# Two-layer hybrid decoder step: PSUM banks of the second mixer dealt 3/3 instead of 4/2, and out-projection norms worked on in PSUM

## The chip, the cores and the metric

The kernel runs on one core of a Trainium2 chip. Its time is device microseconds of one launch, as the median of several runs. The engines are called TensorE (PE), VectorE (DVE), ScalarE (ACT), GpSimd (POOL) and SyncE (SP, which issues the loads and stores).

## What is computed

One step of a decoder of two layers over a prompt of 1024 rows and 8 sample rows, width 1024, all in float32. Layer 0 mixes tokens with forgetting attention (12 heads of 64), layer 1 with differential attention (6 pairs of heads) and rotary positions; in both, four heads attend to a memory. An output projection and a feed-forward part follow, each with a norm before and one behind. The reference, cut to what the change touches:

```python
for i in range(DEPTH):
    xn_p = rms_norm(h_p, g_pre_mix[i])
    ...                                    # layer 1: differential attention
    q, k, v, qm_p = diff_project(xn_p, w_in_diff[j], pos_p)   # q and k with rope
    o_p = diff_head_norm(diff_prompt(q, k, v, lam), g_subln[j], lam_init)
    ...                                    # the same for the sample rows, over a paged cache
def finish_layer(h, o_self, qm, mk, mv, g_post_mix, w_out, g_pre_ffn, g_post_ffn, w_gate_up, w_down):
    merged = jnp.concatenate([o_self, memory_attend(qm, mk, mv)], axis=-1)
    h = h + rms_norm(merged @ w_out, g_post_mix)
    u = rms_norm(h, g_pre_ffn) @ w_gate_up
    f = (silu(u[..., :D_FF]) * u[..., D_FF:]) @ w_down
    return h + rms_norm(f, g_post_ffn)
```

## The kernel before

Every float32 product is made of three: weights and activations are split into a rounded part and a rest (`h_w`, `l_w`; `hi` on ScalarE, L170, and `lo` on VectorE or POOL, L173), and `mm3` runs rounded x rounded, rounded x rest and rest x rounded over eight slices of 128, that is 24 matmuls for each projection tile of 128 columns by a third of the rows (384, 384 and 264).

PSUM has eight banks of 512 columns. In the mixers they are dealt by `MIXER` (L40): one tile of two banks (`s2`, for scores wider than 512), four single banks (`t`: scores up to 512, all transposes, attention outputs `av`, rows turned for the cache), and two for projections (`g`). Tiles of one tag take its banks in turn, so a tile waits until the tile that had the bank before it has been read. In the FFNs another deal holds (`s2` 1, `t` 2, `g` 4); the out projection (`wo`) runs there as well.

The mixer of layer 1 goes head pair by head pair, six in all. For a pair it projects q, k and v, three thirds each (`g`, L1167); between the matmuls, at each call of `beat`, TensorE runs one piece of the attention of the pair before: scores (`s_d`), transposes of the weights (`tp_d`), and the product with v (`av_d`). TensorE's order is written out by `Pinned`: each matmul is pinned behind the one before it in the program. The other engines' orders come from the framework's scheduler.

After a q or k projection VectorE and POOL rotate the tile in place (L998 to L1002), ScalarE copies the rounded part (`qq` L403, `kk` L170) and VectorE writes the rest (`ql` L406, `kk` L173); these are the last readers of the bank. A v tile is read by one ScalarE copy alone (L1175). For attention VectorE takes the row maxima (`nm_d`, L447), ScalarE the exponentials (`p_d`, L463), VectorE merges the two maps (`p_d`, L552), ScalarE drains transposes (`pt_d`, L475), products (`ao_d`, L1191) and turned rows (`tn`, L1137 and L1139). POOL works through the pages of the sample rows' cache beside it all (`kp`, L616).

`finish_tile` (L371) closes a tile of 128 rows: TensorE turns it into the two-bank tile `yp` (eight transposes), ScalarE sums its squares (L338), copies it to SBUF as `yn` (L382, which calls L170), VectorE and POOL form the inverse root (L329, L333), VectorE scales it (L387), adds it to the residual `h` (L388), and, where another part follows, norms it for that (L345) before TensorE turns it back as `xt`. Names begin with `o` for the out projection (18 of them, nine in each layer) and with `f` for the FFN; then come the layer, the third and the tile in it (`y_o002`).

Of the kernel before, what the change touches and what calls it, by code (L numbers as in the profile page):

```python
# [9 lines left out]
F32 = mybir.dt.float32  # L10
# [3 lines left out]
ALU = mybir.AluOpType  # L14
# [3 lines left out]
D = 1024  # L18
# [18 lines left out]
OUTS = 5  # L37
WAIT = 2.5
RD = 9.0
MIXER = {"s2": 1, "t": 4, "g": 2}  # L40
EAGER, IDLE = -200, 400
FFN = {"s2": 1, "t": 2, "g": 4}
THIRDS = ((0, 3, 384), (3, 3, 384), (6, 2, 264))
# [52 lines left out]
class Step:  # L96
# [274 lines left out]
    def finish_tile(self, pool, acc, o, ti, hsrc, hdst, g_post, g_pre, x, name, wait, row=None):  # L371

        nc = self.nc
        r = self.rows(ti)
        h = self.load_h(pool, ti, hsrc, f"h_{name}")
        y = pool.tile([128, D], F32, name=f"yn_{name}", tag="nat")
        if row is None:
            yp = self.b2(f"y_{name}")
            for k in range(8):
                self.pe.transpose(yp[:r, k * 128 : (k + 1) * 128], acc(k)[:, o : o + r], self.ident)  # L380
            ss = self.sumsq(pool, yp[:r], r, y, f"sy_{name}")
            self.hi(y[:r], yp[:r])  # L382
            row = y
        else:
            ss = self.sumsq(pool, row[:r], r, y, f"sy_{name}")
        rs = self.rstd(pool, ss[:r], r, D, f"ry_{name}")
        nc.vector.scalar_tensor_tensor(y[:r], row[:r], rs[:r], g_post[:r], op0=ALU.mult, op1=ALU.mult)  # L387
        nc.vector.tensor_tensor(h[:r], h[:r], y[:r], op=ALU.add)  # L388
        nc.sync.dma_start(hdst(ti), h[:r])
        if x is not None:  # L390
            self.norm(pool, h, r, g_pre, y, name)
            yield wait
            self.to_x(y, r, lambda tv, k0: [(tv, x[:, k0 : k0 + 4])], o, name)
# [647 lines left out]
    def mixer(self, l, xs, st, begin):  # L1041


        nc, io, tc = self.nc, self.io, self.tc
        w_in = io["w_in_fox"][0] if l == 0 else io["w_in_diff"][0]
        self.lag, self.ahead, self.vshare = LAG[l], AHEAD[l], VSHARE[l]
        with ExitStack() as cx:
            self.phase(cx, f"pm{l}", MIXER)
            wp = Weights(self.wpool)
            bufs = {"u4": 12, "p": 2, "pS": 2, "G": 1, "tt": 1}  # L1050
            if l == 1:
# [8 lines left out]
            rs = [{} for _ in range(6)]  # L1060
# [649 lines left out]
```

## Time and profile before

| | |
|---|---|
| runs | 3060.4, 3060.92, 3066.18 us; median 3060.92 us |
| the profiled execution | 3070.34 us, its span 3068.5 us |
| TensorE | busy 2806.3 us (91%), 17567 matmuls |
| VectorE | busy 2068.0 us (67%) |
| ScalarE | busy 1767.4 us (58%) |
| POOL | busy 1107.1 us (36%) |
| mean granted clock of TensorE | 0.963 |

Times within the trace are microseconds from the start of the span. Layer 0 takes the first half, layer 1 begins at some 1550 us; its mixer runs to about 2150 us, and the FFN follows. Busy shares are averages over stages with different limits, so what a place is worth is read from the stage that it lies in: which engine waits there, and for what.

### The profile page before, as it was taken

How to read it: one execution, taken by the hardware profiler on the slowest of the kernel's cores; microseconds unless marked ns; L12 is line 12 of the kernel's file. 1: busy time of each engine (PE TensorE's matmuls, PEld its weight loads, DVE VectorE, ACT ScalarE, POOL GpSimd, SP SyncE). 2: the span in 40 equal slices, each digit the busy share in tenths (PEclk: the TensorE clock that was granted, in tenths of full speed). 3: DMA queues.
4: the chain of work that ended last, by engine and by line, in shares of the span. 5: the costliest groups of instructions: out<-in, count | busy, mean ns of one | idle time of the engine just before them, and what ended most of it. 6: DMA issues, size and time to landing. Idle time of an engine off the chain costs nothing. (4 is left out here: it accounts for less than half of the span.)

```text
span 3068.5 us, 53791 instructions
## 1 busy us (share of the span) xinstructions
PE 2806.3 (91%) x17567; PEld 2647.2 (86%) x17567; DVE 2068.0 (67%) x3645; ACT 1767.4 (58%) x4617; POOL 1107.1 (36%) x840
## 2 busy tenths in 40 slices
PE   7999998878999999999988888888888999999998
PEld 5899998877888998999977878888877899899998
DVE  7566666577678777386466778755887667654655
ACT  6445555444678886355554554465543689864544
POOL 3345556422211111244434556564232111113443
PEclk9999999989999999999999999899998999999999
DMA  5555566486556654356645444464775566644764
GB/s 167 154 154 162 161 170 184 115 263 201 165 184 198 200 191 160 109 164 196 185 148 154 125 124 123 125 179 144 249 229 172 176 226 220 204 148 128 226 180 132
DMA packets 523979, 529.01 MB, mean 172 GB/s; under 512 B 54957, under 2 KB 416078, under 8 KB 523698
## 3 DMA queue, kind: packets, MB, share of 16 engines
q1 hardware_dynamic: 523554, 524.79, 56.2%
q8 instruction: 138, 2.26, 0.3%
q14 instruction: 143, 1.17, 0.1%
q0 software_dynamic: 144, 0.79, 0.1%
HBM read 477.82 MB, written 39.24 MB: 169 GB/s over the span
## 5 line engine op out<-in xcount | busy, mean ns | idle before, releaser
L700 ACT ACTIVATE vp<-vp,s 128x64 f32<-128x64 f32 (+1 forms) x1680 | 462.5, 358 | 119.0 <-DMA vp<-in_cache_fox_v_dram 67.7
L81 PE MATMUL ga<-xf,h_g 128*128 128x384 f32 (+1 forms) x2112 | 499.3, 324 | 0.0
L81 PE MATMUL gu<-xf,h_u 128*128 128x384 f32 (+1 forms) x2112 | 495.1, 321 | 0.0
L81 PE MATMUL g<-xi,h_w 128*128 128x384 f32 (+2 forms) x1728 | 438.7, 340 | 49.7 <-DVE kk L173 23.8
L616 POOL TENSOR_TENSOR kp<-kp,qb 128x768 f32<-128x768 f32 x186 | 344.1, 1852 | 324.5 <-DMA kp<-in_cache_fox_k_dram 140.8
L81 PE MATMUL dn<-h_d,gt 128*128 128x512 f32 x1056 | 352.9, 408 | 20.1 <-ACT gt L170 16.4
L81 PEld LDWEIGHTS ga<-xf,h_g 128*128 128x128 f32 x2112 | 368.2, 191 | 2.0 <-ACT fa L1434 0.2
L81 PEld LDWEIGHTS gu<-xf,h_u 128*128 128x128 f32 x2112 | 365.0, 189 | 0.2
L81 PEld LDWEIGHTS g<-xi,h_w 128*128 128x128 f32 x1728 | 304.5, 197 | 60.8 <-DVE ql L406 26.0
L81 PE MATMUL ga<-xf,l_g 128*128 128x384 f32 (+1 forms) x1056 | 339.4, 321 | 0.0
L81 PE MATMUL gu<-xf,l_u 128*128 128x384 f32 (+1 forms) x1056 | 338.6, 321 | 0.8 <-POOL l_u L173 0.8
L173 POOL TENSOR_TENSOR l_u<-r_u,h_u 128x512 fp32r<-128x512 f32 x96 | 135.1, 1407 | 496.1 <-ACT h_u L170 489.3
L708 DVE TENSOR_TENSOR acc<-acc,vp 128x768 f32<-128x768 f32 x240 | 248.9, 1043 | 77.3 <-ACT vp L700 75.9
L81 PE MATMUL g<-xi,l_w 128*128 128x384 f32 (+2 forms) x864 | 284.9, 330 | 3.8 <-DVE rs_x L329 1.9
L173 POOL TENSOR_TENSOR l_d<-r_d,h_d 128x512 fp32r<-128x512 f32 x96 | 136.1, 1418 | 401.9 <-ACT h_d L170 370.0
L1436 DVE TENSOR_TENSOR fa<-fa,dn 128x512 f32<-128x512 f32 (+1 forms) x400 | 227.5, 578 | 65.3 <-PE dn L81 64.2
L81 PEld LDWEIGHTS dn<-h_d,gt 128*128 128x128 f32 x1056 | 203.7, 194 | 75.9 <-ACT gt L170 20.5
L81 PE MATMUL dn<-l_d,gt 128*128 128x512 f32 x528 | 214.2, 406 | 9.1 <-DVE l_d L173 8.2
L173 POOL TENSOR_TENSOR l_g<-r_g,h_g 128x512 fp32r<-128x512 f32 x96 | 140.6, 1465 | 200.2 <-ACT h_g L170 197.9
L170 ACT ACTIVATE h_u<-r_u 128x512 fp32r<-128x512 f32 x192 | 120.0, 628 | 149.0 <-PE dn L81 59.2
L81 PEld LDWEIGHTS ga<-xf,l_g 128*128 128x128 f32 x1056 | 200.8, 190 | 0.0
L81 PEld LDWEIGHTS gu<-xf,l_u 128*128 128x128 f32 x1056 | 199.1, 189 | 1.1 <-POOL l_u L173 1.0
(590 smaller groups left out, 6305.8 us busy)
## 6 DMA issues: line engine op xcount, KB each, us to landing
kp<-in_cache_fox_k_dram SPq DMA_DIRECT2D x128, 384.0 KB
r_g<-in_w_gate_up_dram SPq DMA_DIRECT2D x192, 256.0 KB
r_u<-in_w_gate_up_dram SPq DMA_DIRECT2D x192, 256.0 KB
r_d<-in_w_down_dram SPq DMA_DIRECT2D x192, 256.0 KB
vp<-in_cache_fox_v_dram SPq DMA_DIRECT2D x128, 384.0 KB
kp<-in_cache_diff_k_dram SPq DMA_DIRECT2D x128, 384.0 KB
vp<-in_cache_diff_v_dram SPq DMA_DIRECT2D x128, 384.0 KB
r_wo<-in_w_out_dram SPq DMA_DIRECT2D x96, 256.0 KB
```

The source lines that it names most:

```text
L81: self.pin(self.eng.matmul(out, w, x, **k), max(n, 256) if x.dtype == F32R else 2 * max(2 * n, 256))
L170: self.nc.scalar.activation(out, src, AF.Copy)
L173: (eng or self.nc.vector).tensor_tensor(out, src, hi.bitcast(F32), op=ALU.subtract)
L616: r = eng.tensor_tensor(k, k, q, op=ALU.mult)
L700: nc.scalar.activation(dst[:, hs], v[:, hs], AF.Copy, scale=wv[:, b, h, g : g + 1])
L708: todo.append(nc.vector.tensor_tensor(acc[b], acc[b], v, op=ALU.add))
L1436: self.last_v = nc.vector.tensor_tensor(dst, dst, o, op=ALU.add).ins.name
```

## The change

`MIXER` becomes a pair, one deal for each layer. Layer 0 keeps one two-bank tile, four single banks and two projection banks; layer 1 has one, three and three. In `finish_tile` the out-projection finishes (names that begin with `o`) no longer copy the turned tile to SBUF: the scaling and the addition read PSUM, and the scaled tile is written back into its bank. The FFN's own finishes stay as they were.

```diff
-MIXER = {"s2": 1, "t": 4, "g": 2}
+MIXER = {"s2": 1, "t": 4, "g": 2}, {"s2": 1, "t": 3, "g": 3}
...
-        y = pool.tile([128, D], F32, name=f"yn_{name}", tag="nat")
+        y = at = pool.tile([128, D], F32, name=f"yn_{name}", tag="nat")
...
             ss = self.sumsq(pool, yp[:r], r, y, f"sy_{name}")
-            self.hi(y[:r], yp[:r])
-            row = y
+            if name[0] == "o":
+
+                row = at = yp
+            else:
+                self.hi(y[:r], yp[:r])
+                row = y
...
-        nc.vector.scalar_tensor_tensor(y[:r], row[:r], rs[:r], g_post[:r], op0=ALU.mult, op1=ALU.mult)
-        nc.vector.tensor_tensor(h[:r], h[:r], y[:r], op=ALU.add)
+        nc.vector.scalar_tensor_tensor(at[:r], row[:r], rs[:r], g_post[:r], op0=ALU.mult, op1=ALU.mult)
+        nc.vector.tensor_tensor(h[:r], h[:r], at[:r], op=ALU.add)
...
-            self.phase(cx, f"pm{l}", MIXER)
+            self.phase(cx, f"pm{l}", MIXER[l])
```

TensorE's order is the same in both kernels. The scheduler orders the other engines anew. (Lines behind the edit are four higher in the changed kernel: L463 is L467 there, L388 is L392.)

ScalarE in layer 1, in the q part of the second head pair; `p_d` are exponentials, `ao_d` and `pt_d` drain single banks (`av_d`, `tp_d`), `qq` is the rounded part of a projection. Before:

```order
L463 ACTIVATE p_d_21636,l_d_21383<-s_d_21624,nm_d_21627 128x384
L463 ACTIVATE p_d_21708,l_d_21381<-s_d_21667,nm_d_21672 128x896
L1191 ACTIVATE ao_d_21696<-av_d_21615,r_d_21374 128x128
L475 ACTIVATE pt_d_21706<-tp_d_21701 128x512
L403 ACTIVATE qq_21389<-g_21584 64x256
L403 ACTIVATE qq_21390<-g_21584 64x256
L1194 ACTIVATE at_d_21698,ss_d_21699<-ao_d_21696 128x128
L1191 ACTIVATE ao_d_21750<-av_d_21748,r_d_21376 128x128
L475 ACTIVATE pt_d_21758<-tp_d_21755 128x256
```

The same place in the changed kernel:

```order
L467 ACTIVATE p_d_21627,l_d_21374<-s_d_21615,nm_d_21618 128x384
L1195 ACTIVATE ao_d_21687<-av_d_21606,r_d_21365 128x128
L1198 ACTIVATE at_d_21689,ss_d_21690<-ao_d_21687 128x128
L479 ACTIVATE pt_d_21697<-tp_d_21692 128x512
L467 ACTIVATE p_d_21699,l_d_21372<-s_d_21658,nm_d_21663 128x896
L1195 ACTIVATE ao_d_21741<-av_d_21739,r_d_21367 128x128
L479 ACTIVATE pt_d_21749<-tp_d_21746 128x256
L407 ACTIVATE qq_21380<-g_21575 64x256
L407 ACTIVATE qq_21381<-g_21575 64x256
```

The drains of `av_d` and `tp_d` (128x512) have moved ahead of the exponentials of 896 columns, and the next two drains ahead of the rounded part of q.

VectorE at the third finish of layer 0 (`o002`): `xf` are the rests of the turned tile of the finish before, `kp` and `sb` cache pages of the sample rows, `l_u` and `l_wo` rests of weights. Before:

```order
L387 SCALAR_TENSOR_TENSOR yn_o002_8955<-yn_o002_8955,ry_o002p_8970,gpm0_8635 128x1024
L620 TENSOR_REDUCE sb_0_9109<-kp7_0_0_9110 128x12
L173 TENSOR_TENSOR xf00_8639<-xt_o0010_9066,xf00_8639 128x4x128
L620 TENSOR_REDUCE sb_0_9109<-kp7_1_0_9161 128x12
L616 TENSOR_TENSOR kp7_2_0_9230<-kp7_2_0_9230,qb7_0_9107 128x768
L173 TENSOR_TENSOR xf00_8639<-xt_o0014_9073,xf00_8639 128x4x128
L388 TENSOR_TENSOR h_o002_8953<-h_o002_8953,yn_o002_8955 128x1024
```

The same place in the changed kernel:

```order
L391 SCALAR_TENSOR_TENSOR y_o002_8954<-y_o002_8954,ry_o002p_8967,gpm0_8635 128x1024
L624 TENSOR_REDUCE sb_0_9106<-kp7_1_0_9158 128x12
L620 TENSOR_TENSOR kp7_2_0_9227<-kp7_2_0_9227,qb7_0_9104 128x768
L173 TENSOR_TENSOR l_wo0171_9142<-r_wo0171_9138,h_wo0171_9140 128x512
L392 TENSOR_TENSOR h_o002_8951<-h_o002_8951,y_o002_8954 128x1024
L620 TENSOR_TENSOR kp7_3_0_9275<-kp7_3_0_9275,qb7_0_9104 128x768
L624 TENSOR_REDUCE sb_0_9106<-kp7_2_0_9227 128x12
L173 TENSOR_TENSOR l_g0001_9212<-r_g0001_9208,h_g0001_9210 128x512
L620 TENSOR_TENSOR kp7_4_0_9321<-kp7_4_0_9321,qb7_0_9104 128x768
L173 TENSOR_TENSOR xf00_8639<-xt_o0010_9063,xf00_8639 128x4x128
```

The addition to the residual, the last reader of the bank, stood behind the two `xf` rests and now stands ahead of them; both operations name the PSUM tile `y_o002` instead of `yn_o002`.

## Rows read from the trace of the kernel before

**Rows 1.** The page: busy us (share of the span) and instructions of each engine.

```profile
PE 2806.3 (91%) x17567; PEld 2647.2 (86%) x17567; DVE 2068.0 (67%) x3645; ACT 1767.4 (58%) x4617; POOL 1107.1 (36%) x840
```

**Rows 2.** Stages of layer 1: length, busy PE, PEld, DVE, ACT, POOL; clock.

```profile
1720.00:1772.00 52.00, 40.54 (x239) 37.69 (x238) 47.30 (x108) 27.36 (x72) 30.31 (x23) 0.93 0.45 126
1772.00:1790.00 18.00, 18.00 (x139) 17.89 (x138) 7.51 (x14) 9.50 (x26) 11.01 (x10) 1.00 0.44 132
1648.00:2013.00 365.00, 313.21 (x1951) 299.49 (x1950) 284.29 (x620) 183.19 (x488) 213.89 (x168) 0.92 0.44 127
```

**Rows 3.** TensorE's waits, 1648 to 2013: us in total, times, longest.

```profile
PE g L81 <- DVE kk L173: 20.5, 10, 5.2
PE g L81 <- DVE ql L406: 15.3, 5, 4.2
PE tp_d L84 <- DVE p_d L552: 12.2, 5, 2.8
```

**Rows 4.** TensorE's timeline: start, length, instruction, idle before it and releaser.

```profile
1743.77 0.94 PE L81 MATMUL g<-xi,h_w 128*128 128x384 f32 x2 [3.39 <-DVE ql L406]
```

**Rows 5.** Four microseconds around that wait and the next four; columns as above.

```profile
1743.00:1747.00 4.00, 3.23 (x13) 3.23 (x13) 3.84 (x9) 1.47 (x3) 0.80 (x2) 0.61 0.87 245
1747.00:1751.00 4.00, 4.00 (x26) 4.00 (x25) 2.31 (x6) 2.60 (x8) 2.82 (x2) 0.96 0.56 172
```

**Rows 6.** Two shorter waits in TensorE's timeline, and the stretches behind them.

```profile
1728.47 0.66 PE L84 MATMUL tp_d<-cm,p_d 128*128 128x128 f32 x4 [2.73 <-DVE p_d L552]
1949.46 0.90 PE L84 MATMUL tp_d<-cm,p_d 128*128 128x128 f32 x3 [2.76 <-DVE p_d L552]
...
1728.00:1732.00 4.00, 3.26 (x19) 2.94 (x20) 3.92 (x11) 2.04 (x5) 0.00 (x0) 1.00 0.18 38
1949.00:1953.00 4.00, 3.54 (x13) 3.54 (x14) 3.92 (x11) 2.04 (x5) 0.00 (x0) 0.50 0.18 40
```

**Rows 7.** A transpose on TensorE and a drain on ScalarE, from their timelines.

```profile
1763.45 0.49 PE L84 MATMUL tp_d<-cm,p_d 128*128 128x128 f32 x3
1764.66 0.49 ACT L1137 ACTIVATE nat<-tn 128x384 f32<-128x384 f32 x1
```

**Rows 8.** The start of the layer in TensorE's timeline.

```profile
1571.01 1.01 PE L81 MATMUL g<-xi,h_w 128*128 128x384 f32 x2 [8.47 <-DVE ql L406]
1587.37 0.98 PE L81 MATMUL g<-xi,h_w 128*128 128x384 f32 x2 [3.37 <-DVE kk L173]
```

**Rows 9.** A finish: timelines of ScalarE and POOL; who VectorE's L387 waits for.

```profile
693.06 1.03 ACT L170 ACTIVATE yn_o<-y_o 128x1024 f32<-128x1024 f32 x1
693.29 0.55 POOL L333 TENSOR_TENSOR ry_o010p<-ry_o,ex 128x1 f32<-128x1 f32 x1 [0.44 <-DVE ry_o L329]
...
  ACT yn_o L170: 6.6, 6
```

**Rows 10.** Finishes: transposes on TensorE and the additions of the finish before.

```profile
642.16 1.03 PE L84 MATMUL y_o<-cm,yo 128*128 128x128 f32 x8
654.27 1.91 PE L84 MATMUL y_o<-cm,yo 128*128 128x128 f32 x8
2227.88 1.04 PE L84 MATMUL y_o<-cm,yo 128*128 128x128 f32 x8
...
642.26 1.97 DVE L388 TENSOR_TENSOR h_o<-h_o,yn_o 128x1024 f32<-128x1024 f32 x1
658.89 2.06 DVE L388 TENSOR_TENSOR h_o<-h_o,yn_o 128x1024 f32<-128x1024 f32 x1
2232.67 1.21 DVE L388 TENSOR_TENSOR h_o<-h_o,yn_o 128x1024 f32<-128x1024 f32 x1
```

**Rows 11.** TensorE's waits in the first finishing stage, 630 to 740.

```profile
PE xt_o L84 <- DVE yn_o L345: 11.5, 2, 8.9
PE xt_o L84 <- DVE ry_o L329: 8.0, 2, 4.9
```

**Rows 12.** The addition L388: count, shortest, median and longest ns.

```profile
L388 DVE TENSOR_TENSOR h_o<-h_o,yn_o x18: 1205/1216/2061, 642.3 to 2828.1; 128x1024 f32<-128x1024 f32 x16, 8x1024 f32<-8x1024 f32 x2
```

## The prediction

> **What bounds the kernel now.** I read the page's busy lines first: TensorE works 91% of the span [rows 1]. So time can only be won where TensorE stands idle or runs at half clock, and the change touches two such places: the second layer's mixer, and the finishing of the out projections at the start of both FFNs. The table by stage comes next. The five head-pair stretches of layer 1 that project q, k and v beside attention take 365 us (73 us a pair); TensorE is busy for 313.21 of them at a mean granted clock of 0.92, VectorE for 284.29 [rows 2]. Then TensorE's waits in that stretch: projections wait 20.5 us in 10 waits for VectorE's `kk` and 15.3 us in 5 for its `ql`, 35.8 us in all, because a `g` bank is only free when the rows of the tile two before it have been rotated and split; attention's transposes wait 12.2 us for `p_d` [rows 3]. Last the timeline: a first matmul of a projection starts at 1743.77 after a wait of 3.39 us [rows 4], and the granted clock of the four microseconds around it is 0.61, of the next four 0.96 [rows 5]: the clock falls from its higher level (2.4 GHz) to its lower (1.2 GHz) after the wait. That costs (1 - 0.61) x 4 + (1 - 0.96) x 4 = 1.7 us on top of the wait. There are two such large waits in a pair, ten in all: 17 us.
>
> **The third projection bank.** It takes away the reason for the 35.8 us and, where it does, for the 17 us: 10.6 us a pair at most, 53 us in all. Not all of it can come, because the bank is late for a reason: VectorE. In the q and k part of the second pair VectorE is busy 47.30 of 52 us, in the v part behind it 7.51 of 18 [rows 2]. The q and k part can shrink by at most the 4.7 us in which VectorE is idle, and those are waits of its own for TensorE, ScalarE and POOL; I take half, 2.4. The other gain is at the start of v: there TensorE waits 3.48 us for `kk` (one of the ten) and loses 1.7 us of clock, with nothing due from VectorE for v itself (ScalarE drains v), and VectorE's late `kk` work then lies in a part where it has 10.5 us idle. With a third bank v's first tile goes into the bank of the first k tile, long free. So 3.5 + 1.7 = 5.2 us there. Sum: 7.6 us a pair. Ends: 0.5 x 5.2 = 2.6 if VectorE's lateness comes back as waits for `s_d` and `p_d`, 10.6 if all goes.
>
> **The single bank that is given up.** Scores up to 512 wide, transposes, attention outputs and natural rows rotate through three banks instead of four. Against the times of before, a tile would wait where the tile three back (not four) is read later than it starts. In the second pair the clearest case is the transpose at 1763.45: the tile three back is drained by ScalarE from 1764.66 to 1765.15, so it would wait 1.7 us [rows 7]; five more lie between 0.15 and 0.6 us, in all about 4 us a pair. ScalarE's new order drains `av_d` and `tp_d` ahead of the next wide `p_d` (the excerpt on ScalarE), so these banks come free earlier, and part of the waits falls on time that TensorE would have spent waiting for VectorE anyway. I take 1.2 of the 4 us, bounds 0 and 4. **Net per pair: 7.6 - 1.2 = 6.4 us, times five = 32 us gained** (bounds: 2.6 - 4 = a loss of 1.4, and 10.6, so -7 to +53).
>
> Around the five pairs the same two edits act once. At the start of the layer the projection waits 8.47 us at 1571.01 and 3.37 us at 1587.37 [rows 8]. Of the first only some 2 us can go, since a finish of the FFN before it (`y_f`) stands in the same TensorE queue and needs its own bank first; the second can go with its 1.7 us of clock; against that some 2 us of new waits on the single banks, where the memory rows are turned. I take 4 us gained (0 to 7). Behind the last pair (memory attention of the prompt, some 75 us) there is no projection to feed, and the tiles of three back are late eight times by 0.2 to 1.6 us: 4 us lost (0 to 8).
>
> **Norms in PSUM.** Eighteen out-projection finishes lose one ScalarE copy each, of 1.03 us [rows 9]. VectorE waited for it six times, 6.6 us in all [rows 9]; but POOL's root, which it needs as well, ends at 693.29 + 0.55 = 693.84 where the copy ends at 693.06 + 1.03 = 694.09, so each such wait gets only 0.25 us shorter, 1.5 us in all, and the other twelve were hidden. In exchange the two-bank tile is held until VectorE's last addition (L388), and there is only one such tile. On the times of before, the second set of transposes, from 642.16, would wait for an addition that ends at 642.26 + 1.97 = 644.23 (2.1 us); the third, from 654.27, for one that ends at 660.95 (6.7 us); the last of the second layer, from 2227.88, for one at 2233.88 (6.0 us) [rows 10]. There are eight such pairs, 14.2 us in the first layer and 15.1 us in the second. But TensorE waits there already: 11.5 and 8.0 us for `yn_o` and `ry_o` of VectorE in the first layer's stage alone [rows 11]. What comes first now, comes later less; and the new order gives `y_o002` its last addition ahead of the `xf` pair instead of behind it (the excerpt on VectorE). VectorE, which bounds that stage, also loses some work. I set the two against each other: **0 us**, with 8 us gained and 15 us lost as ends; the cover is VectorE's lateness, and if it goes, the whole 29 us are to be paid.
>
> L388's addition takes 1.216 us at its median but up to 2.061 us [rows 12]. The Trainium skill ("SBUF — State Buffer", section "Who interferes with whom") says that a VectorE instruction with two SBUF inputs contends with POOL's reads, and one with at most one does not; the changed addition has one. By that rule the stretching would leave the 18 finishes: at most nine of them lie above the median, so at most 9 x 0.85 = 7.6 us, an estimate from the row's spread, and the sum would be lower by as much. I leave it in the range, since what is won by it may be what is lost to the bank.
>
> **Sum.** -32 (five pairs) - 4 (start) + 4 (tail) + 0 (finishes) = -32 us. The profiled execution takes 3070.34 us, so it would become 3038; the median of the runs lies 9.4 us below that execution (3060.92), and I subtract the same 32 us there: **3029 us**.
>
> **Rivals.**
>
> All goes: every `g` wait and every fall of the clock behind one vanishes, and ScalarE's new order covers the single banks. Gain 53 + 4 = 57 us: 3004 us. Against it stands VectorE's 47.30 of 52 us. Chance 0.08.
>
> VectorE is the bound: TensorE gets ahead by one bank and then stands at `s_d` and `p_d` as long as it stood at `g`; only the start of v gains, half of it. Gain 2.6 x 5 = 13 us, less 3 for single banks: 10 us, 3051 us. For it speaks the 47.30 us, against it the idle 10.5 us in every v part. Chance 0.13.
>
> The clock doesn't come back: waits of 3.4 us turn into more and shorter ones, but the clock still falls. A wait of 2.73 us at 1728.47 left the clock at 1.00, one of 2.76 us at 1949.46 was followed by 0.50 [rows 6], so shorter waits can go either way. Without the 17 us of clock the gain is 32 - 17 = 15 us: 3046 us. Chance 0.12. The Trainium skill ("TensorE: Matmul & The Clock Gate", section "A second HAM failure mode: psum-queue depth-cycling") describes this case: short idle times between groups of matmuls that cycle through PSUM banks make the clock go down and up. The two rows agree with it half the time.
>
> Slower: the finishes' bank. If VectorE does not catch up at the first FFN tiles, the 14.2 + 15.1 us are paid in full, and four of the eight waits are over 5 us long, each with a fall of the clock worth 1.7 us: 36 us. With the mixer at 24 us of gain instead of 32 that is 12 us slower: 3073 us. The point from which it decides: when TensorE's waits for `yn_o` and `ry_o` stay as long as they are although the `y_o` transposes start later. Against it: those waits sit right behind. Chance 0.07.
>
> That the banks are not what the diff says can hardly be: TensorE's order is the same row for row, and only the bank of a tile differs.
>
> **How the numbers follow.** The forecast's own case (a gain of 18 to 48 us) has 0.55, the rivals 0.08, 0.13, 0.12 and 0.07, and 0.05 is left for mixtures that end near zero. What a measurement of this kernel can tell from no change is about 0.2%, 6 us. Faster: 0.55 + 0.08 + 0.12 and 0.10 of VectorE's 0.13 = 0.85. Same: the other 0.03 and the 0.05 = 0.08. Slower: 0.07. The range leaves out most of the first rival below and the slower and near-zero cases above: 3003 to 3053 us.
>
> **What would show it.** Right: the stretch of five pairs falls from 365 to some 333 us, the waits of `g` for `kk` and `ql` in it go below 8 us, its clock rises to 0.95 or more, and waits for ScalarE's drains appear at `tp_d` and `av_d`, 1 to 4 us a pair. Wrong: waits for `p_d` grow from 12.2 us to 25 or more (VectorE's bound); the clock stays near 0.92 with the `g` waits gone; `y_o` transposes show waits for L392 of more than 5 us while the waits for `yn_o` stay (the slower case). The forecast fails if VectorE's idle time in the v parts can't take the overhang.

## The result, and the profile after

The changed kernel takes 3030.77 us (median; 3021.57 to 3034.49) against 3063.55 us before: the ratio is 0.9886, with a 95% interval of 0.9857 to 0.9916, so it is faster by some 35 us. The forecast was 3029 us, within 3003 to 3053. Beside later experiments it was run once more: 0.9877 [0.9852, 0.9902].

TensorE executes the same 17567 matmuls in the same order in all these kernels, so a stretch can be measured between the starts of the same two instructions in two traces. All stage lengths below are taken like that.

| stage (first and last instruction in the trace of before) | before | after | forecast | found |
|---|---|---|---|---|
| up to the start of layer 1 (10.9 to 1552.3), of it the first finishes and 60 us behind (632.9 to 800.1) | 1541.4; 167.1 | 1530.8; 157.8 | 0 | -10.6; -9.3 |
| start of layer 1 (1552.3 to 1647.9) | 95.6 | 91.9 | -4 | -3.7 |
| five head-pair stretches (1647.9 to 2012.8) | 364.9 | 335.3 | -32 | -29.6 |
| tail of the mixer (2012.8 to 2090.1) | 77.3 | 82.2 | +4 | +4.9 |
| finishes of layer 1 and 100 us behind (2159.0 to 2360.1) | 201.1 | 200.4 | 0 | -0.7 |
| out projection of layer 1, remaining FFN and end | 769.7 | 766.2 | 0 | -3.5 |

These come from one profiled execution each. The first mixer, up to 550 us, is the same code in both and took between 539 and 550 us in the profiles of twelve kernels here that leave it alone, so single stages can differ by several us for no reason. The same goes for the stages that gain. The changed kernel was profiled once more, and there its five pairs took 339.2 us, not 335.3; in eight profiles of kernels with the third bank they took 335 to 339 us, in the two with the old deal 365 and 364. The first finishes with the 60 us behind took 163 to 167 us in four kernels with the old norms and 156 to 159 in nine with the new norms or a variant of them, so the 9.3 us of the table lie at the upper end of a gain of some 6. The stages add up to 42 us, more than the 33 us between the medians, since the profiled execution of before was a long one (3070.34 us) and that of the changed kernel a short one (3027.93).

First the five pairs. The table by stage of the changed kernel (length, busy PE, PEld, DVE, ACT, POOL, granted clock) stands against [rows 2]:

```profile
1634.00:1970.00 336.00, 302.60 (x1954) 286.51 (x1954) 283.05 (x623) 183.09 (x491) 214.63 (x168) 0.97 0.47 137
```

The stretch is 29 us shorter, TensorE is busy for 10.6 us less with the same matmuls (302.60 against 313.21), because the clock is granted at 0.97 instead of 0.92 (it is at its lower level twelve times in the stretch before and six times in the changed one), and VectorE's work is the same within 2 us, pressed into less time. Where it goes is seen in the second pair, from the first matmul of q to the first of v and from there to the next pair; before:

```profile
1716.40:1768.10 51.70, 40.28 (x247) 37.40 (x244) 45.76 (x108) 27.22 (x74) 28.88 (x24) 0.96 0.44 123
1768.10:1789.00 20.90, 20.86 (x145) 20.79 (x146) 10.62 (x19) 9.60 (x26) 13.91 (x12) 0.93 0.46 140
```

and after:

```profile
1697.00:1742.90 45.90, 39.77 (x246) 37.34 (x246) 41.50 (x93) 23.80 (x64) 24.63 (x21) 0.96 0.39 112
1742.90:1764.80 21.90, 20.01 (x148) 19.29 (x147) 15.31 (x32) 12.61 (x35) 18.59 (x15) 1.00 0.63 178
```

Over all five pairs the q and k parts shrink from 258.0 to 220.4 us, with 229.0 and 204.1 us of VectorE's work in them; the v parts grow from 107.4 to 115.3 us, and VectorE's work in them from 55.6 to 79.2. TensorE's waits in the whole stretch (total, times, longest), against [rows 3]:

```profile
PE tp_d L84 <- DVE p_d L556: 10.6, 5, 2.7
PE av_d L81 <- ACT nat L1141: 9.6, 5, 2.8
PE s_d L81 <- ACT p_d L467: 6.2, 10, 2.1
PE tp_d L84 <- ACT ao_d L1195: 4.0, 5, 1.0
PE tn L84 <- ACT pt_d L479: 1.1, 5, 0.2
PE tn L84 <- ACT p_d L467: 1.0, 1, 1.0
PE g L81 <- DVE kk L173: 0.5, 1, 0.5
```

Of the 35.8 us that projections waited for `kk` and `ql`, 0.5 us is left. What is new are the lines with `nat`, `ao_d` and `pt_d` and the `tn` line for `p_d`: waits for a single bank that ScalarE has not read yet, 9.6 + 4.0 + 1.1 + 1.0 = 15.7 us. The waits of `s_d` for `p_d`, 3.8 us before, are 6.2.

Then the finishes, against [rows 11]: TensorE's waits from 632 to 742 in the changed kernel.

```profile
PE y_o L84 <- DVE h_o L392: 12.3, 3, 6.6
PE xt_o L84 <- DVE yn_o L345: 3.7, 1, 3.7
PE mp L84 <- DVE xf L173: 2.7, 1, 2.7
PE xt_o L84 <- DVE mt L173: 1.7, 1, 1.7
PE xt_o L84 <- DVE ry_o L329: 0.9, 1, 0.9
```

The held bank costs 12.3 us of waiting, and the waits of `xt_o` for `yn_o` and `ry_o` fall from 19.5 to 4.6 us. The same happens in layer 1 (`y_o` 14.1 us; `xt_o` for the two from 19.2 to 0.4 us). The addition, against [rows 12] (count, shortest, median and longest ns):

```profile
L392 DVE TENSOR_TENSOR h_o<-h_o,y_o x18: 1202/1212/1222, 645.7 to 2784.4; 128x1024 f32<-128x1024 f32 x16, 8x1024 f32<-8x1024 f32 x2
L392 DVE TENSOR_TENSOR h_f<-h_f,yn_f x18: 1203/1224/2306, 1327.4 to 3022.1; 128x1024 f32<-128x1024 f32 x16, 8x1024 f32<-8x1024 f32 x2
```

None of the 18 additions with a PSUM operand is stretched any more, while their 18 twins in the FFN finishes, which read two SBUF tiles, still reach 2306 ns. That is what the Trainium skill's rule on two SBUF inputs says ("SBUF — State Buffer", section "Who interferes with whom"); the trace agrees, 1222 against 2306 ns. The short times are no lack of work on POOL: it was at work during eight of the 18 additions, and these took 1206 to 1222 ns; it was at work during eight of the 18 twins too, and seven of those took 1589 to 2306.

### The profile page after: what moved, and what is told of

It reads as the page before. It is cut to its first block, busy times and chain, and to the rows that moved or that the text cites. A ratio compares the mean times of both kernels' runs of the same rounds, so it can differ in the third digit from the quotient of the medians.

```text
span 3026.2 us, 53779 instructions
## 1 busy us (share of the span) xinstructions
PE 2794.9 (92%) x17567; PEld 2634.6 (87%) x17567; DVE 2055.2 (68%) x3645; ACT 1750.4 (58%) x4599; POOL 1103.1 (36%) x840
## 5 line engine op out<-in xcount | busy, mean ns | idle before, releaser
L81 PE MATMUL g<-xi,h_w 128*128 128x384 f32 (+2 forms) x1728 | 428.4, 334 | 2.3 <-DVE mkk L173 0.5
L81 PEld LDWEIGHTS dn<-h_d,gt 128*128 128x128 f32 x1056 | 201.1, 191 | 71.5 <-ACT gt L170 16.5
L170 ACT ACTIVATE h_u<-r_u 128x512 fp32r<-128x512 f32 x192 | 120.0, 628 | 146.6 <-PE dn L81 60.0
```

Source lines behind the costliest of these rows:

```text
L81: self.pin(self.eng.matmul(out, w, x, **k), max(n, 256) if x.dtype == F32R else 2 * max(2 * n, 256))
L170: self.nc.scalar.activation(out, src, AF.Copy)
```

## The experiments

Ratios are to the kernel before on the same chip, with their 95% intervals. The changed kernel's own are 0.9886 [0.9857, 0.9916] and 0.9877 [0.9852, 0.9902]. Banks only, norms only, seven banks and the scaled tile in SBUF were timed on one chip; turns first, both kernels with the lighter VectorE and the changed kernel again on a second; both mixers, the copy kept and all finishes in PSUM on a third. The changed kernel itself was not timed on the first and third. Its four variants there came out at 0.9925 to 0.9935, whatever the edit, so their 12 to 18 us above it may be the chip's, and no loss against it is shown by these times alone.

### One part at a time

Banks only: `MIXER` and `MIXER[l]` as in the change, `finish_tile` as before.

> Only the second layer's mixer gets three projection banks and three single banks; the finishes copy the turned tile to SBUF as before. Theory (the third projection bank gives nearly all of the gain): -29 to -35 us against the kernel before, and the five head-pair stretches take about 335 us instead of 365, as in the changed kernel. Rival (the norms in PSUM give some 9 us of it, the amount by which the changed kernel's profile is ahead before the second mixer begins): -20 to -26 us, and nothing ahead of 1550 us in the trace.

Measured: 0.9929 [0.9909, 0.9950], 22 us faster. The five pairs take 336.6 us, the start of the layer 93.0, the tail 82.9; at the first finishes it takes 163.5 us against 167.1, within the spread of the old norms, and TensorE still waits 5.3 us for the sample rows' maxima there. The third bank gives about two thirds of the gain, not all of it; in time the rival's number is right, and the mixer's part of the profile is the theory's.

Norms only: the change with `MIXER` as before for both layers.

> Only the finishes of the out projections work in PSUM; both mixers keep four single and two projection banks. Theory (TensorE's new waits for the two-bank tile replace the waits for xt that were there): 0 us, within 4, with waits of y_o for the addition of 10 us or more in each finishing stage and the waits of xt_o down by as much. Rival (the freed copy and the shorter additions speed VectorE's queue up): -6 to -12 us, the same 8 us at 740 to 800 us as in the changed kernel's profile. Second rival (the bank costs more than it gives): +4 us or more.

Measured: 0.9967 [0.9949, 0.9985], 10 us faster. The five pairs take 364.4 us, as before; the first finishes with what is behind them take 159.0 us against 167.1. The waits did change places as expected (12.3 us for the bank), but the theory's 0 us falls: the rival holds in its size. Where it is gained can be seen in TensorE's waits behind the finishes: from 740 to 800 us in the kernel before,

```profile
PE dn L81 <- DVE l_d L173: 5.5, 1, 5.5
PE smt_d L84 <- DVE r_d L846: 5.0, 1, 5.0
```

and at the same place (749 to 799) with the norms alone in PSUM:

```profile
PE dn L81 <- DVE l_d L173: 3.6, 1, 3.6
PE mb_d L81 <- DVE r_m L850: 0.4, 1, 0.4
```

`smt_d` is the transpose of the sample rows' row maxima `r_d`, which VectorE forms at the end of a long queue. VectorE is late there, and in the changed order it is less late, 140 us behind the first `y_o`: the wait is gone. Between the matmuls that start at 739.99 and 800.09 in the kernel before lie 60.1 us there and 50.4 with the norms alone; TensorE waits 10.6 and 4.0 us of it and is busy 49.5 and 46.4, at a clock of 0.89 and 0.97. Two excerpts of VectorE's timeline (kernel before, then changed) with the first `y_o` at 632.90 and at 636.46:

```profile
775.16 0.55 DVE L1401 TENSOR_TENSOR sg<-sg,gu 128x384 f32<-128x384 f32 x1
775.62 0.68 DVE L173 TENSOR_TENSOR l_g<-r_g,h_g 128x512 fp32r<-128x512 f32 x1
776.29 0.56 DVE L173 TENSOR_TENSOR gt<-sg,gt 128x384 fp32r<-128x384 f32 x1
780.36 1.75 DVE L846 TENSOR_REDUCE r_d<-s 128x96 f32<-128x1536 f32 x1
```

```profile
775.07 1.75 DVE L850 TENSOR_REDUCE r_d<-s 128x96 f32<-128x1536 f32 x1
776.74 0.54 DVE L1405 TENSOR_TENSOR sg<-sg,gu 128x384 f32<-128x384 f32 x1
779.06 0.68 DVE L173 TENSOR_TENSOR l_g<-r_g,h_g 128x512 fp32r<-128x512 f32 x1
780.26 0.54 DVE L173 TENSOR_TENSOR gt<-sg,gt 128x384 fp32r<-128x384 f32 x1
```

From the first `y_o` to the end of `r_d` it is 780.36 + 1.75 - 632.90 = 149.2 us before and 775.07 + 1.75 - 636.46 = 140.4 us after. With the old norms it was 145.9 and 146.6 us in two more kernels, with the new ones 143.0 and 143.4: some 5 us on the mean. Not all of that is work saved. The six additions of this stage take 7.3 us together instead of 8.5 to 9.4, and the scheduler has put three operations of the FFN (`sg`, `l_g`, `gt`, 1.8 us) behind `r_d` that stood ahead of it. No run here separates the new order from the saved work. In layer 1 nothing is gained in the same way: the finishes and the 100 us behind them take 201.1 us before, 200.4 and 201.8 in the changed kernel and 201.1 with the norms alone.

The single bank alone: three single banks, two for projections, one bank unused, old norms.

```diff
-MIXER = {"s2": 1, "t": 4, "g": 2}
+MIXER = {"s2": 1, "t": 4, "g": 2}, {"s2": 1, "t": 3, "g": 2}
```

> The second mixer gives up its fourth single bank and gets nothing for it: three single and two projection banks, one bank unused; finishes as before. This prices the single bank alone. Theory (its waits fall mostly on time in which TensorE would wait for VectorE anyway, as long as the projection waits are there): +2 to +10 us in all, and the projections still wait about 30 us for kk and ql. Rival (the waits are paid in full, 4 us a pair and 4 us in the tail): +20 us or more.

Measured: 1.0020 [1.0007, 1.0033], 6 us slower, the theory's case; no single stage of its profile shows where. The five pairs take 364.7 us, no more than before, though waits for single banks are there. The stage from 1647 to 2012,

```profile
1647.00:2012.00 365.00, 310.62 (x1952) 292.72 (x1952) 288.79 (x624) 183.43 (x490) 214.33 (x170) 0.95 0.44 128
```

and TensorE's waits in it:

```profile
PE g L81 <- DVE ql L406: 14.3, 5, 4.3
PE tp_d L84 <- DVE p_d L552: 12.2, 5, 2.8
PE g L81 <- DVE kk L173: 12.2, 13, 2.7
PE tp_d L84 <- ACT nat L1137: 7.6, 5, 1.6
```

The new 7.6 us for `nat` come out of the waits for `kk`, which fall from 20.5 us to 12.2, the longest from 5.2 to 2.7 us; with more and shorter waits for `kk`, the clock is 0.95 instead of 0.92. While the projections are late anyway, the single bank costs the pairs nothing.

### Why the projection bank was late

The kernel before and the changed kernel with less work for VectorE: in layer 1 each page's products are summed over 8 columns of 64.

```diff
-k.rearrange("p (h d) -> p h d", d=64), axis=AX, op=ALU.add
+k.rearrange("p (h d) -> p h d", d=64)[:, :, : 64 if l == 0 else 8], axis=AX, op=ALU.add
```

> The kernel before, with less work for VectorE in the second mixer: each page of the sample rows' keys is summed over 8 columns of 64 (the sample rows' scores of the second layer are wrong, nothing else), about 13 sums of 0.95 us a pair become about 0.2 us, 10 of VectorE's 57 us. Theory (the projections wait for a bank because VectorE is late): the waits of g for kk and ql fall from 35.8 us to below 15 us and the five pairs from 365 to 345 us or less. Rival (the wait is the length of the chain of rotation and split through VectorE, POOL and ScalarE, not VectorE's load): the waits stay above 28 us and the pairs above 357 us.

> The changed kernel with the same lighter VectorE in the second mixer. Theory (with the third bank VectorE's load is what is left between 335 us and TensorE's own some 295 us): the pairs fall from 335 to 320 us or less. Rival (the single banks that ScalarE drains are what is left): the pairs stay above 328 us.

Measured: 0.9845 [0.9820, 0.9870] and 0.9802 [0.9774, 0.9831]; part of that lies outside the pairs, where the same sums are made. With two projection banks the five pairs take 334.7 us, with three 333.5; the changed kernel's profile on this chip has 339.2. Waits from 1635 to 1969 in the first,

```profile
PE g L81 <- DVE kk L173: 11.4, 6, 3.9
PE s_d L81 <- ACT p_d L463: 10.6, 11, 2.0
PE g L81 <- DVE ql L406: 6.6, 5, 1.4
PE tp_d L84 <- DVE p_d L552: 3.8, 5, 1.1
```

and from 1624 to 1958 in the second:

```profile
PE s_d L81 <- ACT p_d L467: 12.5, 12, 2.0
PE tp_d L84 <- ACT nat L1142: 10.0, 5, 2.9
PE av_d L81 <- ACT nat L1142: 4.4, 3, 2.0
PE tp_d L84 <- DVE p_d L556: 4.4, 5, 1.2
```

So taking 43 us off VectorE (241.60 us busy in that stretch instead of 284.29) gains the 30 us in the pairs that a third bank gains, without one: the bank was late because VectorE was. The waits for `kk` and `ql` fall to 18.0 us, not below 15 as I had expected. With the third bank, the lighter VectorE adds 2 to 6 us (333.5 against 335.3 and 339.2): there the theory falls and the rival holds, since what is left then are banks that ScalarE drains (`p_d`, `nat`: 26.9 us).

The tail belongs to this as well. It grew from 77.3 to 82.2 us with the change (82.9 with the banks only), and with the lighter VectorE it is 75.5 us with two projection banks and 76.1 with three. So the growth depends on VectorE's load: part of the gain is given back there. The 79.2 us that it takes with seven banks do not price the single bank, since it takes 79.0 with the norms alone and the old deal. VectorE is no busier in the tail than before (45.9 us against 48.3); TensorE waits longer for `p_d` (4.4 us against 2.8) and is busy longer, 68.9 us against 65.8, at a clock of 0.96 against 0.98.

ScalarE's drains of the turned k rows set ahead of its other work, in the changed kernel:

```diff
-self.spawn(natural(a, t, hp, f, r), RD if a == 1 and l == 1 else 4.0)
+self.spawn(natural(a, t, hp, f, r), RD if a == 1 and l == 1 else 4.0, EAGER if a == 1 and l == 1 else 0)
```

> The changed kernel with one order changed: ScalarE drains the turned k rows (tn, to nat) ahead of what else it has ready, in the second mixer only. In the changed kernel's profile TensorE waits 9.6 us for that drain, five times, one in each pair, since the bank three tiles back is still unread. Theory (these waits are what is left of the single bank that was given up): the five waits go and the time falls by 3 to 9 us. Rival (they cover time in which VectorE would be late anyway): the waits move to p_d or the projections and the time stays within 2 us.

> The changed kernel itself, beside the three runs below on the same chip. Theory: about 0.989 of the kernel before, as before; if its two parts simply add up it is the banks' 0.993 times the norms' 0.997, 0.990.

Measured: 0.9893 [0.9870, 0.9916], and 0.9877 [0.9852, 0.9902] for the changed kernel beside it: no difference that can be told. The waits for `nat` fall only to 7.1 us (9.6 and 10.4 in the two profiles of the changed kernel), and others take their place (1630 to 1967):

```profile
PE tp_d L84 <- DVE p_d L556: 12.0, 5, 2.8
PE s_d L81 <- ACT p_d L467: 11.1, 16, 2.3
PE av_d L81 <- ACT nat L1141: 7.1, 5, 2.9
PE tp_d L84 <- ACT ao_d L1195: 4.1, 5, 1.0
PE g L81 <- DVE kk L173: 3.8, 5, 2.1
```

The rival holds as far as the intervals tell. The changed kernel measured again is also where banks and norms, multiplied, would put it: 0.9929 x 0.9967 = 0.990.

The 3/3 deal in the first layer's mixer too:

> The changed kernel with the 3/3 deal in the first layer's mixer as well. There the projections are not rotated: in the profile of before no projection waits for kk or ql up to 550 us, VectorE is not late, and a v or k tile leaves its bank soon. Theory (the third projection bank pays only where VectorE is late with the rotated tiles): no gain, and up to 8 us lost to the fourth single bank: 0.988 to 0.992 of the kernel before. Rival (three and three is simply the better deal for a stream of projections between attention): 5 us or more gained in the first 550 us.

Measured: 0.9935 [0.9916, 0.9955], above both ratios of the changed kernel, though on another chip. The first mixer takes 553.0 us in its profile, above the 539 to 550 of all others. There was no wait for `kk` or `ql` to remove, and TensorE's waits for exponentials and drained banks grow (up to 640 us: `s_f` 3.3 us against 1.8, `tp_m` 4.1 against 2.3, `xt_x` for `xi` 5.3 against 1.3). The rival falls: nothing is gained. A loss is likely but its size open: the first mixer is 9 us above the mean of the others and 3 above the longest, and the 16 us by the ratios are between chips.

### What in the norms counts

The changed kernel, but the scaled tile written to SBUF:

```diff
-                row = at = yp
+                row = yp
```

> The changed kernel with one thing different: the scaling of the out projection's norm reads PSUM but writes SBUF, so the two-bank tile is free 2 to 4 us earlier, at the scaling and not at the addition; the addition reads two SBUF tiles again. If the held bank costs time: the waits of y_o fall from 12.3 and 14.1 us to below 8 us in each finishing stage and the time is 2 to 6 us below the changed kernel's. If the addition's second SBUF input costs time: additions of up to 2 us come back and the time is equal or up to 5 us higher. If VectorE's queue sets the stage in both, the time is the same within 2 us.

Measured: 0.9928 [0.9904, 0.9951], above both ratios of the changed kernel, though its interval touches the first one's. The waits of `y_o` do fall, to 3.5 and 6.5 us, but the waits of `xt_o` come back; TensorE's waits in the first finishing stage (640 to 750),

```profile
PE xt_o L84 <- DVE yn_o L345: 12.1, 3, 7.1
PE y_o L84 <- DVE yn_o L391: 3.5, 2, 1.8
PE xt_o L84 <- DVE ry_o L329: 3.5, 2, 2.4
```

and the addition (columns as above):

```profile
L392 DVE TENSOR_TENSOR h_o<-h_o,yn_o x18: 1206/1218/2107, 652.2 to 2811.7; 128x1024 f32<-128x1024 f32 x16, 8x1024 f32<-8x1024 f32 x2
```

Freeing the bank earlier gains nothing that can be seen; the stretched additions, up to 2107 ns, are back. So the first theory is not borne out. The second is not shown either, though the ratios put the kernel some 14 us above the changed one: that is between chips, and the gain behind the first finishes is still there. `r_d` ends 143.3 us after the first `y_o`, as with the norms in PSUM, `smt_d` waits 2.3 us for it (5.0 to 5.3 with the old norms), and the stage takes 158.5 us (157.8 and 159.4 in the two profiles of the changed kernel). In layer 1 the finishes take 210.9 us, 9 to 10 more than in the changed kernel, but the kernel with all finishes in PSUM, whose code there is the changed kernel's, has 208.6.

The copy kept, the scaled tile in PSUM:

```diff
+            self.hi(y[:r], yp[:r])
+            row = y
             if name[0] == "o":
-                row = at = yp
-            else:
-                self.hi(y[:r], yp[:r])
-                row = y
+                at = yp
```

> The changed kernel with ScalarE's copy of the turned tile kept: the scaling reads SBUF and writes PSUM, the addition reads PSUM. It keeps the short additions and gives the wait for the copy back. Theory (of the 6 us that VectorE's queue gains before the sample rows' softmax in the first layer, about half is the wait for the copy and half the additions that are no longer stretched): the maxima r_d end about 143 to 146 us after the first y_o (140 to 143 in the changed kernel, 146 to 149 with the old norms), and the time is 2 to 6 us above the changed kernel's. Rival (the additions are all of it): within 2 us of the changed kernel.

Measured: 0.9925 [0.9912, 0.9938]. Profile and times disagree here. In the profile `r_d` ends 140.5 us after the first `y_o`, as in the changed kernel, and the first finishes with what follows take 155.7 us (157.8 there): by that the copy gives nothing on top of the short additions (1198 to 1214 ns), the rival's case. But they need not be what gives the gain, since the scaled tile in SBUF keeps most of it with long ones; in both variants, too, one or two of the three FFN operations are ordered behind `r_d`. The times say 0.9925 against 0.9886 and 0.9877, some 13 us slower. Those come from other chips, and I don't know where the difference would lie. What in the norms counts (the additions, the copy, or VectorE's new order) stays open.

All turned finishes in PSUM, the last third's `y_f` included (`if True:` in place of `if name[0] == "o":`):

> The changed kernel with the last third's FFN finishes (six tiles, y_f) in PSUM too. At the end of the kernel nothing covers the held bank: each tile's transposes would wait for the addition of the tile before, some 5.5 us a tile (1.0 transposes, 1.0 squares, 0.2 and 0.6 for the root, 1.3 scaling, 1.2 addition) instead of 3.3. Theory (the bank costs what is uncovered): 3 to 5 us slower at the end, 0 to 4 us at the start of the second layer, the time 3 to 9 us above the changed kernel's. Rival (the dropped copy is worth more than the bank everywhere): equal or faster.

Measured: 0.9933 [0.9914, 0.9952], above both ratios of the changed kernel. At the end of the kernel nothing covers the held bank (from 3000 us; the kernel before shows 4.5 us there, in two waits of 2.3 for ScalarE's copy):

```profile
PE y_f L84 <- DVE h_f L392: 9.4, 2, 4.7
```

That is 4.9 us more waiting at the end, within the 3 to 5 expected, and the price of the bank in the open, two waits of 4.7 us. Under the out projection's finishes the same bank's waits took the place of waits for VectorE that were there before. The start of layer 1 takes 90.3 us, so nothing is lost there. By the ratios the kernel is 14 to 17 us above the changed one, more than the 3 to 9 expected; beyond the end's 4.9 us no place for it is shown, and the chip is another.

## Why the prediction was right, and where its terms were off

The total was right: 32 us forecast, about 35 found, in the direction and by the main mechanism named. That it came so near is partly luck: by time the banks alone gave 22 us where 32 were forecast for them, and the norms alone 10 us where none was. Step by step:

- **Where the time lies.** The waits for `kk` and `ql` with the clock behind them were the place: -29.6 us in the pairs against -32 (-25.7 by the second profile of the changed kernel). The waits fell as forecast to below 8 us (0.5), the stretch to 335 us (333 forecast), the clock to 0.97 (0.95 or more).
- **The gain of the third bank, 7.6 us a pair: too small.** The waits gave 35.3 / 5 = 7.1 us a pair, and TensorE's busy time, which holds the clock, 10.6 / 5 = 2.1 us: 9.2 us together. I had let only half of VectorE's idle time in the q and k part shrink. In fact VectorE's idle time over the pairs fell from 365 - 284.29 = 81 us to 336 - 283.05 = 53 us. The cap that I drew from 47.30 of 52 us was no cap, since VectorE's work itself can leave the q and k part: 24 us of it ran on into the five v parts. The time was gained up to the first matmul of v (258.0 to 220.4 us), and the v parts, which I had getting shorter by the clock, grew by 8 us in all, where `av_d` now waits 9.6 us for `nat`.
- **The single bank, 1.2 us a pair: too small too.** Its waits measured 15.7 / 5 = 3.1 us, close to the 4 that the comparison with the tile three back gave. The reason that I gave for taking less, that the waits fall on time spent waiting anyway, is what the seven banks show while the projections still wait; with those waits gone the cover is gone with them, and I priced it with the cover. The two errors, +1.6 and -1.9 us a pair, cancel by luck: 6.4 forecast, 5.9 found.
- **The clock** came back only in part as time: 10.6 us less busy, where I counted ten falls of 1.7 us; there were twelve, and six are left. Waits of up to 2.7 us for `p_d` remain, and [rows 6] had shown that the clock may fall behind these.
- **Start and tail**, -4 and +4: found -3.7 and +4.9. In the tail the size was right and the reason is not shown: with the lighter VectorE the third bank costs it only 0.6 us, so VectorE's load has a part in it.
- **The finishes, 0 us: the step that failed.** The exchange of waits was as forecast, and the new waits, 12.3 and 14.1 us, were covered. But I asked only what TensorE waits for inside the finishing stage. VectorE's queue does not end with it: it reaches the sample rows' softmax some 150 us after the first `y_o`, TensorE waits there too, and VectorE's gain of some 5 us comes out at that place: -8.6 us at 740 to 800 us in this profile, -10 us by time for the norms alone (interval 5 to 16), at or beyond the 8 us that I had put as the bound of a gain. Of the stretching, 7.6 us at most by my estimate, 4.2 went (all 18 additions took 26.0 us and take 21.8). In this stage the shorter additions give 1.2 to 2.1 of the 5 us, three operations ordered elsewhere 1.8, and the rest is not told apart.
- **The rivals.** "VectorE is the bound" is right for the kernel before and wrong for the changed one. "The clock doesn't come back" did not happen (0.97). "Slower by the bank" did not happen at the finishes; the case at the kernel's end, with 4.7 us a wait, shows what the bank costs where no other wait covers it.

## What to carry to other kernels

Before moving a buffer from one use to another, look for what empties it late: a bank that a saturated engine empties is worth a bank more, or work less for that engine, and the two don't add up. The price of the bank that is given up must be read with the waits gone that the change removes, not with them in place. And where the engine that saves work is the late one, follow its queue beyond the stage, to the next point at which the main engine waits for it, and compare its order there too: an edit that gives the scheduler a new order changes more than the work. A variant that is to be compared within a few us needs its rival on the same chip.

## What had not been expected of the hardware

An addition on VectorE of 1024 columns with one PSUM operand took 1202 to 1222 ns in all 18 cases, eight of them beside POOL at work; with two SBUF operands the same addition reached 2061 to 2293 ns at most in the five kernels that kept it. With seven banks TensorE's waits for `kk` were more and shorter (13 of up to 2.7 us in place of 10 of up to 5.2), and its granted clock was 0.95 instead of 0.92 over 365 us, at the same length of the stretch and almost the same busy time: so a deal of banks can change the clock without changing the time. It is one profile, and the longest wait alone does not decide: with the norms alone the longest was 3.5 us and the clock 0.93.
